# One sequence at a time in the compression stage of a hybrid decoder step, the first sequence's leading tokens asked for ahead of its others

## The chip, the core and the metric

The kernel runs on one core of one Trainium2 chip. The metric is the device time of one execution in microseconds (us): the kernel before takes 1231.15 us, the median of 3 runs (1231.12 to 1231.8). The core has four engines that compute, each with an instruction stream of its own: TensorE (PE in the profile; its weight loads are shown apart as PEld), VectorE (DVE), ScalarE (ACT) and GpSimd (POOL). SyncE (SP) only issues transfers here, and ACT and POOL can issue transfers too. The transfers of all three run on the same 16 DMA engines.

## The reference, cut to what matters

The whole program is one step of a decoder layer (two kinds of attention, gates, an MLP) for a prompt of 512 tokens and for 8 sample sequences, each with 2048 tokens in a paged cache of 16 pages of 128 tokens. The change touches the first stage alone, in which the cached raw keys and values of the 8 sequences are compressed:

```
def compress_blocks(x, pos, w1, w2):            # x: 8 x 2048 tokens x 2 groups x 64
    xc = x.reshape(b, n_chunk, 16, NSA_GROUPS, HEAD_DIM)          # chunks of 16 tokens
    w1 = w1.reshape(2, 16, HEAD_DIM, CMP_HIDDEN)                  # CMP_HIDDEN = 128
    lead  = einsum('bncgd,cdh->bngh', xc + pos[0], w1[0])
    trail = einsum('bncgd,cdh->bngh', xc + pos[1], w1[1])
    return einsum('bngh,hd->bngd', silu(lead[:, :-1] + trail[:, 1:]), w2)
```

It is done once for keys (`k`) and once for values (`v`), with a weight `w1` of 2048 x 128 each. The result is needed only in a later stage (the sample attention); what follows the first stage directly is the projection of the 576 new tokens by `w_in` (`z` in the profile).

## The kernel before, in words

**Data.** A sequence's pages are loaded into a tile `cpg` of 2 MB (16 loads of 128 KB, a page each; 4 such tiles, so that sequence b + 4 waits for the tile of sequence b). A page lies over 8 partition groups of 16 partitions, 8 tokens to a partition. The page's number in the cache is data: `by_page` (L157) first loads 8 page numbers into registers of the engine that issues (L162), then issues 8 loads (through `dma`, L151 to L155).

**Units.** The work is cut into units (L548) of one token place j (0 to 3; tokens 2j and 2j + 1 of each 8) and one of k or v. A unit of a sequence is made so:

- `cmp_order` (L447): DVE copies tokens 2j, 2j + 1 of a sequence into an order fit for transposing (`ro`; one copy serves k and v, so one for every two units).
- `rows_turn` (L456): four TensorE transposes (`ct`) into one PSUM bank, then twice ACT rounds half of it (`xh`) and DVE forms the remainder (`xl`), so that a product of full precision is had from three products of rounded numbers. Two `ring` buffers hold the results of two units.
- `cmp_hidden` (L473): 12 matmuls (`hid`) of the unit's `w1` parts with `xh` and `xl`, added up over all four j in PSUM.
- `cmp_taps` (L372), for the first eight units alone: ACT and DVE split the unit's part of `w1` in the same way (`w1hlk`, `w1hlv`, 128x512 each).

Before the change sequences 0 and 1 go through in units of one sequence (256 columns a matmul, units 0 to 15), and 2 to 7 in three pairs (512 columns, units 16 to 39; a pair's unit has two `ro` copies, eight transposes and four `xh` and `xl`).

**Order.** PE's order is the order of the program: every PE instruction is chained to the one before (`link`, L87). In the loop of `first_stage` (L623) it is: transposes of unit u + 1, matmuls of unit u, then whatever `todo[u]` holds: norms of the new tokens and their transposes (`norm`, `turned`; `nt` in the profile), the adaLN products (`ada_first`; `ada`, `adat`), the second weights of the compression (`cmp_act`, `cmp_out`, `cmp_keys`; `co`, `kct`), page loads of later sequences. On the other engines a planner orders what is not pinned; `behind()` (L535) pins an instruction behind the latest `xh` and `xl` of the program. The copy `ro` that opens a new sequence or pair is always so pinned, behind the `xh` and `xl` of the unit before it (L636 to L639). The other copies are pinned for units below 16 only.

**Transfers.** Each issuing engine's transfers go in the program's order (L153). At the start SP loads the page table, 8 pages of sequence 0, then sequences 1, 2 and 3; ACT loads `w1` of k (2 x 512 KB), the other 8 pages of sequence 0, then `w1` of v; POOL loads small constants.

**The seam.** At unit 38 of 40 `seam()` (L2095) opens the next stage: the first part of `w_in` (`winr`, two halves) is split into `winh`, `winl`, and the eight rows of the normed input into `h2_0` to `h2_7` (`split_pack`, one ACT and two DVE instructions each; `h` in the profile, L777). Rows 0 to 2 are pinned behind unit 38's `xl`, the others and both halves of `w_in` behind unit 39's. The first `z` tile needs all eight rows and both halves, in order.

Of the kernel before, what the change touches and what calls it, by code (L numbers as in the profile page):

```python
# [45 lines left out]
class Step:  # L46
# [465 lines left out]
    def first_stage(self, pl, pe, hf, seam):  # L512


        nc = self.nc
        self.chain = ""
        self.sideb = self.mmb
# [23 lines left out]
        def pinned(f):  # L541
            def g():
                with behind():
# [25 lines left out]
        ada, ends = [4, 0, 5, 1, 6, 2, 7, 3], {}  # L569
        todo = {u: [] for u in range(40)}  # L570
        todo[9] += [pinned(self.ada_silu)]
# [17 lines left out]

        todo[8] += [pages(4)]  # L590
        todo[9] += [asked(self.cmp_second)]
        todo[14] += [pages(5)]
        todo[15] += [asked(load_x)]
        todo[16] += [load_x, load_x]
        todo[17] += [asked(wada(0))]
        todo[19] += [load_x]
        todo[21] += [load_x]
        todo[23] += [asked(wada(1))]
        todo[24] += [self.late_loads]
        todo[20] += [pages(6)]  # L600
        todo[22] += [pages(7)]
        for k, u in enumerate((22, 25, 27, 29, 31, 32, 34, 35)):
            todo[u] += [lambda k=k: ends.update({k: self.ada_first(pe, ada[k])})]
            todo[u + 1] += [lambda k=k: ends[k]()]
            if k > 1:
                todo[(23, 26, 28, 30, 32, 33)[k - 2]] += [wada(k)]
            if k % 2:
                todo[max(u + 2, 28)] += [lambda k=k: self.modulate(0, hf, range(k - 1, k + 1))]
        self.lfg = {}
        for y, u in enumerate((25, 28)):  # L610
            todo[u] += [pinned(lambda y=y: self.stage_logf(pe, y))]
            todo[u + 2] += [lambda y=y: self.store_logf(y)]
        for i in range(3):
            for kv in range(2):
                todo[8 * i + 14 + kv] += [lambda i=i, kv=kv: self.cmp_act(pl, i, kv)]
        for i in range(3):
            for kv in range(2):
                todo[8 * i + 18 + kv] += [lambda i=i, kv=kv: self.cmp_out(pl, i, kv)]
            todo[8 * i + 21] += [lambda i=i: self.cmp_keys(i)]
        self.cmp_order(pl, 0)  # L620
        self.cmp_taps(0)
        self.rows_turn(0)
        for u in range(40):  # L623
            if u % 2 == 0 and u + 2 < 40 and (u + 2) % 8:
                with behind() if u + 2 < 16 else nullcontext():
                    self.cmp_order(pl, u + 2)
            if u + 1 < 8:
                with behind():
                    self.cmp_taps(u + 1)
            if u + 1 < 40:  # L630
# [5 lines left out]
            if (u + 2) % 8 == 0 and u + 2 < 40:  # L636

                with behind():
                    self.cmp_order(pl, u + 2)  # L639
# [1433 lines left out]
    def run(self):  # L2073
# [21 lines left out]
        def seam():  # L2095
# [158 lines left out]
```

## Time and profile before

| what | value |
|---|---|
| measured runs | 1231.12, 1231.15, 1231.8 us |
| the profiled execution | 1231.5 us |
| its span (first to last instruction) | 1229.7 us, 1.8 us less |
| granted TensorE clock, mean | 0.994 |
| first transposes of unit 0 | at 18.68 us |
| last `hid` matmul, begin of `z` | 170.66 and 170.88 us |
| moved to and from memory | 188.11 MB |

All times below are from the span's start. A row of a timeline has the start, the duration, engine, line, operation, what it writes <- what it reads, the number of instructions merged in the row and, in brackets, how long the engine had been idle and what released it. The chain of waits is followed back from the last instruction: each row is a start, a duration and what the end of the program was waiting for. A table by stretches has, for each stretch, the busy time of each engine with its number of instructions, the granted clock, the mean busy share of the DMA engines (shares over 1 come from overlapping packets) and GB/s. The duration of a matmul has its way through the array in it; what a stream of them costs is read from start to start.

### The profile page before, as it was taken

What the parts mean: (1) busy time and instruction counts of PE and PEld (TensorE: products, weight loads), DVE (VectorE), ACT (ScalarE), POOL (GpSimd) and SP (SyncE); (2) the same over time, 40 slices, a digit from 0 to 9 for tenths busy, and PEclk for the clock granted to TensorE, in tenths of its full rate; (3) what the DMA queues carried; (4) which work ended last, traced back from release to release, by engine and by line L of the source; (5) the groups of instructions that cost most, each with busy time, mean ns of one, the idle gap of its engine ahead of it and who ended that gap; (6) DMA issues with size and microseconds to landing.
All of it is one profiled execution on the core that took longest, in us unless ns stands there. A gap on an engine that the chain in (4) does not pass through costs nothing.

```text
span 1229.7 us, 24815 instructions
## 1 busy us (share of the span) xinstructions
PE 1186.9 (97%) x9475; PEld 1022.7 (83%) x9475; DVE 684.9 (56%) x1875; ACT 513.6 (42%) x1152; POOL 131.2 (11%) x144
## 2 busy tenths in 40 slices
PE   3899999999999989999999999999999999999998
PEld 3888789999666556666799999998989989899896
DVE  3688785676788845555543445654343433434546
ACT  2455453454777744454432333365423213232230
POOL 1012100001211120000200000001102011020110
PEclk9999999999999899999999999999999999999999
DMA  9589547794866449789763234115314223142202
GB/s 208 160 246 272 161 145 235 245 319 151 287 208 200 132 138 308 255 264 295 172 165 94 78 93 128 29 52 155 103 43 130 69 70 103 53 119 70 69 18 77
DMA packets 170201, 188.11 MB, mean 153 GB/s; under 512 B 16185, under 2 KB 149762, under 8 KB 167906
## 3 DMA queue, kind: packets, MB, share of 16 engines
q1 hardware_dynamic: 157890, 167.13, 44.6%
q0 software_dynamic: 6880, 16.25, 4.4%
q10 hardware_dynamic: 5312, 3.15, 1.2%
q8 instruction: 75, 1.23, 0.4%
q14 instruction: 44, 0.36, 0.1%
HBM read 176.48 MB, written 30.90 MB: 169 GB/s over the span
## 4 chain that ended last, share of the span: by engine, by line
PE 85%; DVE 5%; DMA 4%; SPq 3%; ACT 2%; issue 1%; DVEq 0%; ACTq 0%
PE up L77 17%; PE dn L77 17%; PE mg L77 8%; PE z L77 7%; PE hid L77 5%; PE wo L77 4%; PE br L77 4%; PE ss L77 4%; SPq L155 3%; PE k L83 2%; PE ct L83 2%; PE so L77 2%; DMA cpg<-in_cache_nsa_kv 2%; PE ada L77 1%; PE sp L83 1%
## 5 line engine op out<-in xcount | busy, mean ns | idle before, releaser
L77 PE MATMUL z<-winh,h 128*128 128x264 f32 (+1 forms) x576 | 111.0, 286 | 0.3
L2024 POOL TENSOR_TENSOR u<-u 128x576 f32<-128x576 f32 x32 | 53.4, 1669 | 409.3 <-ACT u L112 318.2
L77 PEld LDWEIGHTS z<-winh,h 128*128 128x128 f32 x576 | 91.7, 190 | 2.1 <-DVE h L777 0.9
L77 PE MATMUL z<-winl,h 128*128 128x264 f32 (+1 forms) x320 | 88.2, 284 | 0.2 <-DVE winl L131 0.2
L100 DVE TENSOR_TENSOR acc<-acc,dn 128x512 f32<-128x512 f32 x60 | 39.8, 685 | 73.0 <-PE dn L77 73.0
L77 PE MATMUL mg<-hH,wmh 128*128 128x288 f32 x256 | 75.9, 298 | 2.0 <-ACT wmh L112 2.0
L77 PE MATMUL mg<-hH,wml 128*128 128x288 f32 x256 | 75.9, 298 | 0.9 <-DVE wml L131 0.9
L112 ACT ACTIVATE xh<-ct 128x256 fp32r<-128x256 f32 x128 | 48.0, 385 | 59.2 <-PE ct L83 35.8
L77 PE MATMUL mg<-hL,wmh 128*128 128x288 f32 x256 | 72.6, 294 | 0.0
L131 DVE TENSOR_TENSOR xl<-ct,xh 128x256 fp32r<-128x256 f32 x128 | 51.6, 420 | 19.4 <-ACT xh L112 17.7
L777 DVE TENSOR_TENSOR u<-u,u 128x512 fp32r<-128x512 f32 x64 | 27.4, 469 | 60.7 <-ACT u L112 60.7
L77 PEld LDWEIGHTS z<-winl,h 128*128 128x128 f32 x320 | 60.6, 190 | 0.4 <-DVE winl L131 0.4
L83 PE MATMUL ct<-identF,ro 128*128 128x128 f32 x256 | 36.3, 281 | 22.7 <-DVE ro L115 22.1
L83 PEld LDWEIGHTS ct<-identF,ro 128*128 128x128 f32 x256 | 29.6, 146 | 26.6 <-DVE ro L115 18.7
L77 PEld LDWEIGHTS mg<-hH,wmh 128*128 128x128 f32 x256 | 48.6, 190 | 2.4 <-ACT wmh L112 2.2
L77 PEld LDWEIGHTS mg<-hH,wml 128*128 128x128 f32 x256 | 48.5, 189 | 1.1 <-DVE wml L131 1.1
L131 DVE TENSOR_TENSOR wml<-wmr,wmh 128x1024 fp32r<-128x1024 f32 x14 | 17.1, 1224 | 56.0 <-ACT wmh L112 55.9
L112 ACT ACTIVATE u<-up 128x256 f32<-128x256 f32 (+1 forms) x96 | 27.8, 325 | 48.7 <-PE up L77 48.7
L77 PEld LDWEIGHTS mg<-hL,wmh 128*128 128x128 f32 x256 | 47.2, 188 | 0.1
L77 PE MATMUL hid<-xh,w1hlk 128*128 128x512 f32 (+1 forms) x160 | 45.0, 369 | 0.1
L77 PE MATMUL hid<-xh,w1hlv 128*128 128x512 f32 (+1 forms) x160 | 43.9, 360 | 0.5 <-ACT xh L112 0.5
L1700 DVE CUSTOM_DVE_ANT_0 sS<-ss,scr 128x512 f32<-128x512 f32 x32 | 22.1, 691 | 30.2 <-PE ss L77 30.2
(951 smaller groups left out, 3584.1 us busy)
## 6 DMA issues: line engine op xcount, KB each, us to landing
adw<-in_w_ada SPq DMA_DIRECT2D x16, 1024.0 KB
foxD<-in_cache_fox_kv SPq DMA_DIRECT2D x128, 128.0 KB
wur<-in_w_up SPq DMA_DIRECT2D x32, 512.0 KB
wdr<-in_w_down SPq DMA_DIRECT2D x32, 512.0 KB
cpg<-in_cache_nsa_kv SPq DMA_DIRECT2D x120, 128.0 KB
fr<-foxD SPq DMA_DIRECT2D x28, 512.0 KB
sr<-in_cache_nsa_kv SPq DMA_DIRECT2D x112, 128.0 KB
wada<-in_w_ada POOLq DMA_DIRECT2D x8, 1024.0 KB, 6.3
```

The costliest lines, as they stand in the source:

```text
L77: ins = self.nc.tensor.matmul(out, a, b, start=start, stop=stop, skip_group_check=True)
L83: ins = self.nc.tensor.transpose(out, in_, self.identF[:n, :n])
L100: self.nc.vector.tensor_tensor(out, a, b, op=op)
L112: return self.nc.scalar.activation(out, in_, f, **kw)
L131: self.splits.append((eng or self.nc.vector).tensor_tensor(l, x, h.bitcast(F32), op=OP.subtract).ins)
L155: self.issued[eng] = getattr(self.nc, eng).dma_start(out, in_).ins
L777: self.packed = (eng or self.nc.vector).tensor_tensor(h2[:, o:o + n], x[:, i:i + n], h2[:, i:i + n].bitcast(F32), op=OP.subtract).ins
L1700: self.nc.vector.tensor_tensor_reduce(self.S[u], pb, self.ramp[:, 512 * i:512 * i + 512], 1.0, LOW, OP.add, OP.max, self.stat[b][0][:, i / ...
L2024: nc.gpsimd.tensor_tensor(u[j], u[j], u[j], op=OP.mult)
```

## The change

All 8 sequences become units of one sequence: 64 units of 256 columns instead of 16 of 256 and 24 of 512. `w1` is loaded by token place (8 loads of 256 KB instead of 4 of 512 KB): places 0 and 1 by ACT, 2 and 3 by POOL. Of sequence 0 the first two tokens of each page's 8 are asked for first (SP and ACT, 8 pages each, 32 KB a load), the other six after (SP and POOL, 96 KB a load). The copies `ro` are all pinned behind the latest `xl`. The entries of `todo` are moved to the new numbering. At the seam, now at unit 62 of 64, row 0 is pinned behind unit 61's `xl`, row 1 behind unit 62's, the others behind unit 63's.

```diff
@@ by_page
-                    engines=[{"sync": mybir.EngineType.SP, "scalar": mybir.EngineType.Activation}[eng]],
+                    engines=[{"sync": mybir.EngineType.SP, "scalar": mybir.EngineType.Activation,
+                              "gpsimd": mybir.EngineType.Pool}[eng]],
@@ cmp_raw
-        n = "kv"[kv]
-        raw = pe.tile([P, 16, P], F32, tag="big", bufs=2, name=f"w1raw{n}")
-        for j in (0, 8):
-            self.dma("scalar", raw[:, j:j + 8], self.I[f"cmp_w1_{n}"][0, P * j:P * j + D].rearrange("(j p) h -> p j h", p=P))
-        self.w1raw.append(raw)
+        self.w1raw.append(pe.tile([P, 16, P], F32, tag="big", bufs=2, name=f"w1raw{kv}"))
+
+    def cmp_raw_taps(self, kv, js, eng="scalar"):
+        v = self.I[f"cmp_w1_{'kv'[kv]}"][0].rearrange("(a j p) h -> j p a h", a=4, p=P)
+        for j in js:
+            self.dma(eng, self.w1raw[kv].rearrange("p (a j) h -> p a j h", a=4)[:, :, j], v[j])
@@ first_stage
-        self.units = [(b // 2, bs, j, kv) for b, bs in ((0, (0,)), (1, (1,)), (2, (2, 3)), (4, (4, 5)), (6, (6, 7)))
-                      for j in range(4) for kv in range(2)]
+        self.units = [(b // 2, (b,), j, kv) for b in range(NB) for j in range(4) for kv in range(2)]
+        N = len(self.units)
...
-        self.cmp_raw(pe, 0)
+        for kv in range(2):
+            self.cmp_raw(pe, kv)
+            self.cmp_raw_taps(kv, (0,))
...
-        self.cmp_pages("sync", 0, slice(0, 8))
-        self.cmp_pages("scalar", 0, slice(8, 16))
-        self.cmp_raw(pe, 1)
+        self.cmp_pages("sync", 0, slice(0, 8), slice(0, 2))
+        self.cmp_pages("scalar", 0, slice(8, 16), slice(0, 2))
+        self.cmp_pages("gpsimd", 0, slice(8, 16), slice(2, 8))
+        self.cmp_pages("sync", 0, slice(0, 8), slice(2, 8))
+        for j in range(1, 4):
+            for kv in range(2):
+                self.cmp_raw_taps(kv, (j,), "scalar" if j == 1 else "gpsimd")
...
-        for k, u in enumerate((19, 21, 23, 25, 27)):
-            todo[u - 2] += [lambda k=k: norm(k)]
+        for k, u in enumerate((22, 26, 30, 34, 38)):
+            todo[u - 3] += [lambda k=k: norm(k)]
             todo[u] += [lambda k=k: turned(k)]
...
-        for k, u in enumerate((22, 25, 27, 29, 31, 32, 34, 35)):
+        for k, u in enumerate((29, 34, 39, 43, 47, 50, 53, 56)):
             todo[u] += [lambda k=k: ends.update({k: self.ada_first(pe, ada[k])})]
             todo[u + 1] += [lambda k=k: ends[k]()]
...
-                todo[8 * i + 14 + kv] += [lambda i=i, kv=kv: self.cmp_act(pl, i, kv)]
+                todo[16 * i + 14 + kv] += [lambda i=i, kv=kv: self.cmp_act(pl, i, kv)]
...
-        for u in range(40):
-            if u % 2 == 0 and u + 2 < 40 and (u + 2) % 8:
-                with behind() if u + 2 < 16 else nullcontext():
+        for u in range(N):
+            if u % 2 == 0 and u + 2 < N and (u + 2) % 8:
+                with behind():
                     self.cmp_order(pl, u + 2)
...
-            if u == 37:
-                self.behind38 = self.splits[-1], self.last_high
-            if u == 38:
+            if N - 4 <= u < N - 2:
+                self.ahead.append((self.splits[-1], self.last_high))
+            if u == N - 2:
                 seam()
@@ run, in seam
-            rows(self.behind38, range(3))
+            rows(self.ahead[0], (0,))
+            rows(self.ahead[1], (1,))
             for i in range(2):
                 self.win_split(self.pw, 0, i, last)
-                rows(last, ((3, 4), (5, 6, 7))[i])
+                rows(last, ((2, 3, 4), (5, 6, 7))[i])
```

The cut lines move the other loads of `todo` (pages of sequences 4 to 7 at units 8, 14, 22, 30 instead of 8, 14, 20, 22; the input rows, the adaLN weights, the forget values) in the same way.

More of the change, by code (lines that the diff above doesn't have):

```diff
@@ L515, in first_stage @@
         nc = self.nc
-        self.chain = ""
+        self.chain, self.ahead = "", []
         self.sideb = self.mmb
@@ L569, in first_stage @@
         ada, ends = [4, 0, 5, 1, 6, 2, 7, 3], {}
-        todo = {u: [] for u in range(40)}
+        todo = {u: [] for u in range(N)}
         todo[9] += [pinned(self.ada_silu)]
@@ L588, in asked @@
             return g
-        todo[8] += [pages(4)]
+        for b in range(4, NB):
+            todo[8 * (b - 4) + (8 if b == 4 else 6)] += [pages(b)]
         todo[9] += [asked(self.cmp_second)]
-        todo[14] += [pages(5)]
         todo[15] += [asked(load_x)]
[L594 to L601, printed above, removed]
-        for k, u in enumerate((22, 25, 27, 29, 31, 32, 34, 35)):
+        todo[16] += [load_x]
+        todo[18] += [load_x]
+        todo[20] += [asked(wada(0))]
+        todo[23] += [load_x]
+        todo[25] += [asked(wada(1))]
+        todo[27] += [load_x]
+        todo[28] += [self.late_loads]
+        for k, u in enumerate((29, 34, 39, 43, 47, 50, 53, 56)):
             todo[u] += [lambda k=k: ends.update({k: self.ada_first(pe, ada[k])})]
             todo[u + 1] += [lambda k=k: ends[k]()]
-            if k > 1:
-                todo[(23, 26, 28, 30, 32, 33)[k - 2]] += [wada(k)]
+            if k < 6:
+                todo[u + 1] += [wada(k + 2)]
             if k % 2:
-                todo[max(u + 2, 28)] += [lambda k=k: self.modulate(0, hf, range(k - 1, k + 1))]
+                todo[max(u + 2, 40)] += [lambda k=k: self.modulate(0, hf, range(k - 1, k + 1))]
         self.lfg = {}
-        for y, u in enumerate((25, 28)):
+        for y, u in enumerate((36, 41)):
             todo[u] += [pinned(lambda y=y: self.stage_logf(pe, y))]
-            todo[u + 2] += [lambda y=y: self.store_logf(y)]
+            todo[u + 4] += [lambda y=y: self.store_logf(y)]
         for i in range(3):
             for kv in range(2):
-                todo[8 * i + 14 + kv] += [lambda i=i, kv=kv: self.cmp_act(pl, i, kv)]
+                todo[16 * i + 14 + kv] += [lambda i=i, kv=kv: self.cmp_act(pl, i, kv)]
         for i in range(3):
             for kv in range(2):
-                todo[8 * i + 18 + kv] += [lambda i=i, kv=kv: self.cmp_out(pl, i, kv)]
-            todo[8 * i + 21] += [lambda i=i: self.cmp_keys(i)]
+                todo[16 * i + 18 + kv] += [lambda i=i, kv=kv: self.cmp_out(pl, i, kv)]
+            todo[16 * i + 21] += [lambda i=i: self.cmp_keys(i)]
         self.cmp_order(pl, 0)
@@ L629, in first_stage @@
                     self.cmp_taps(u + 1)
-            if u + 1 < 40:
+            if u + 1 < N:
                 self.rows_turn(u + 1)
-            if u == 37:
-                self.behind38 = self.splits[-1], self.last_high
-            if u == 38:
+            if N - 4 <= u < N - 2:
+                self.ahead.append((self.splits[-1], self.last_high))
+            if u == N - 2:
                 seam()
-            if (u + 2) % 8 == 0 and u + 2 < 40:
+            if (u + 2) % 8 == 0 and u + 2 < N:
                 with behind():
```

## The prediction

> **What bounds the kernel now.** I read the shares of the chain of waits first, then the stage's stretches, then the chain through them.
>
> ```profile
> PE 85%; DVE 5%; DMA 4%; SPq 3%; ACT 2%; issue 1%; DVEq 0%; ACTq 0%
> ```
> ```profile
> 4.00:26.00 22.00, 7.18 (x36) 6.65 (x37) 5.31 (x11) 4.20 (x10) 2.92 (x6) 1.00 1.15 235
> 26.00:58.00 32.00, 28.92 (x289) 27.63 (x288) 20.00 (x47) 14.43 (x35) 1.30 (x3) 1.00 0.54 158
> 61.64:171.06 109.42, 109.11 (x712) 87.96 (x713) 87.62 (x304) 56.66 (x135) 15.43 (x21) 1.00 0.71 201
> ```
> ```profile
> 2.95 0.72 SPq L155
> 3.86 6.62 DMA cpg<-in_cache_nsa_kv
> ...
> 28.21 0.58 SPq L155
> ...
> 53.90 0.54 SPq L155
> 54.62 0.54 SPq L155
> 55.35 2.65 DMA cpg<-in_cache_nsa_kv
> 58.39 0.52 DVE ro L115
> ...
> 61.64 1.06 PE ct L83 x8
> ...
> 77.79 0.87 PE nt L83 x8
> ...
> 83.19 0.87 PE ct L83 x8
> 84.06 2.79 PE hid L77 x12
> ...
> 96.43 0.45 PE nt L83 x4
> ```
>
> PE is the bound, but not at first. Until 26 us the DMA engines are full (share 1.15). Until 55 us SP asks for one page each 0.72 us, and the first pair waits for sequence 3's last page. From 61.64 to 171.06 PE is busy for 109.11 of 109.42 us: there only more work or a new gap on PE can change the end. A pair's unit costs 0.87 + 2.79 = 3.66 us.
>
> **The change part by part.** First the units of one sequence and the starts of sequences, on PE (first two fences, the first from the opening stretch, the second later) and on DVE:
>
> ```profile
> 18.68 1.97 PE L83 MATMUL ct<-identF,ro 128*128 128x128 f32 x8 [18.68 <-DVE ro L115]
> ...
> 23.57 0.85 PE L83 MATMUL ct<-identF,ro 128*128 128x128 f32 x4
> ...
> 26.01 0.60 PE L83 MATMUL ct<-identF,ro 128*128 128x128 f32 x4
> ```
> ```profile
> 34.53 0.60 PE L83 MATMUL ct<-identF,ro 128*128 128x128 f32 x4
> ...
> 38.06 0.63 PE L83 MATMUL ct<-identF,ro 128*128 128x128 f32 x4 [1.48 <-DVE ro L115]
> 39.94 0.60 PE L83 MATMUL ct<-identF,ro 128*128 128x128 f32 x4
> ...
> 43.71 0.60 PE L83 MATMUL ct<-identF,ro 128*128 128x128 f32 x4
> ```
> ```profile
> 54.61 0.60 PE L83 MATMUL ct<-identF,ro 128*128 128x128 f32 x4
> ...
> 57.80 0.63 PE L83 MATMUL ct<-identF,ro 128*128 128x128 f32 x4 [1.14 <-DVE ro L115]
> 59.23 0.63 PE L83 MATMUL ct<-identF,ro 128*128 128x128 f32 x4 [0.79 <-DVE ro L115]
> ```
> ```profile
> 56.60 0.42 DVE L131 TENSOR_TENSOR xl<-ct,xh 128x256 fp32r<-128x256 f32 x1 [0.45 <-ACT xh L112]
> 56.97 0.69 DVE L115 COPY ro<-cpg 128x1024 f32<-128x1024 f32 x1
> ```
>
> *Width.* From 39.94 to 43.71 two single units take 3.77 us against 3.66 for a pair's: 24 x 0.11 = 2.6 us more, and one set of four transposes (0.44, half of 0.87) is still to come at the point from which I count (unit 17's transposes, begun at 61.64 before): **+3.1**. ACT and DVE instructions stay the same in number.
>
> *Front.* Before, unit 0 starts at 18.68, when all of sequence 0 and k's `w1` have landed, some 3.1 MB. Units 2 to 7 need these same bytes still (sequence 0, and places 0 and 1 of `w1`), at the same full DMA engines; SP's 16 shorter loads take it to 2.95 + 16 x 0.72 + 0.7 for page numbers = 15.2 us, and a landing behind that (2.65 at 55.35, 6.62 at 3.86), 17.9 to 21.8. Unit 0 and perhaps 1 go ahead of it: 2.95 + 8 x 0.72 + 2.65 + 0.7 for `ro` is 12 us at the earliest. So unit 2's transposes start at 18.7 to 22.5 instead of 23.57 (in the first rows above; unit 3 followed at 26.01, a pitch and a wait for v's `w1` later): I take 20.4, a gain of 3.2, and 0.4 for that wait: **-3.6**, bounds -1.5 and -5.5. SP's eight more loads cost nothing while it waits for full DMA engines anyway (24 loads until 28.21 are 1.05 us each); with that cover gone they would cost 8 x 0.72 = 5.8 us, sequence 1 would land at 28.8 + 2.65 + 5.8 = 37 instead of 31, and unit 8, due at 34.4, would take back all of the gain. POOL's eight page loads and four of `w1` go ahead of its constants, each at 0.5 to 0.9 us by these rows, so some 11 us and one wait; the constants are needed at 45. A page load by POOL with a register the trace doesn't show: 0.5 to 2 us each, and 0.5, the nearest row, is taken; at 2 the tokens of pages 8 to 15 come at 21, which is the range's end above.
>
> ```profile
> 8.29 0.52 POOL L155 DMA_DIRECT2D gains<-in_nsa_qn_g  x1 [2.40 <-DMA adw<-in_c_prompt]
> ...
> 67.84 0.92 POOL L155 DMA_DIRECT2D wada<-in_w_ada  x1 [0.45 <-ACT xh L112]
> ```
>
> The Trainium skill ("DMA: Bandwidth & Descriptors", "Issuing engines are not separate DMA queues") says that transfers started from several engines share the same 16 and that this saves only the time of asking. The share of 1.15 until 26 us agrees. By that rule alone the front would give nothing, and the sum below would be 3.6 us higher; it is a rival below.
>
> *The wait for sequence 3.* Unit 16 needs sequence 2 alone. Before, unit 16 starts at 57.80 and unit 17 at 61.64; now 1.88 later: 3.84 - 1.88 = **-2.0**. Sequences 3 to 7 then have 13 us each of asking for 17 of PE, so SP isn't late again.
>
> *The gap at each new sequence.* The copy that opens a sequence stands behind the last `xl`: 54.61 transposes, 56.60 `xl`, 56.97 `ro`, 57.80 next transposes. That is 3.19 us where the steady pitch is 1.88, a gap of 1.3 on PE; from 34.53 to 38.06 it is even 3.53. A pair hid it behind 2.79 us of matmuls; now there are only 1.44 (1.88 - 0.44). Five more such starts follow (units 22, 30, 38, 46, 54). What `todo` holds there fills part: 0.87 at 22, 0.87 and 0.22 at 30, 0.45 at 38, 0.22 at 54, nothing at 46 (the 0.22 is half of the 0.45 row, two transposes for four). What is left: 0.43 + 0.21 + 0.85 + 1.3 + 1.08 = 3.9; before lost some 0.6 at pairs: **+3.3**, bounds 0 and 6.
>
> *Chain within a unit.* Transposes, `xh`, `xl`, `xh`, `xl` last from 54.61 to 57.0, 2.4 us. They must end before the next unit's sixth matmul, 1.88 + 0.36 + 0.6 = 2.84 later, so a DVE or ACT instruction over some 0.4 us between them reaches PE; a pair had over 1 us. What comes between:
>
> ```profile
> L131 DVE TENSOR_TENSOR xl<-ct,xh 128x256 fp32r<-128x256 f32 x93 | 37.2, 419 | 5.5 <-ACT xh L112 4.0
> L115 DVE COPY ro<-cpg 128x1024 f32<-128x1024 f32 x21 | 14.6, 712 | 1.0 <-PE ct L83 0.9
> ```
>
> DVE's 87.6 us less 96 x 0.42 and 24 x 0.70 are 30 us of other work over 48 units, 0.64 us each. Bounds: with 0.69 us of DVE and 0.62 of ACT more per unit (the `w1` splits), 26.01 to 34.53 took 8.52 for four units instead of 7.54, 0.25 a unit: 48 x 0.25 = 12. From 38.06 to 54.61, seven units with 3.2 us of other PE work, it cost 0.1 in all: 0. PE's other work, 109.4 - 87 = 22 us, gives the chain time in many units, but not where norms, `cmp_act` and the modulation of rows fall. I take 30% of the upper end: **+3.5**.
>
> *Seam.* DVE's rows around it, then PE's:
>
> ```profile
> 168.57 1.26 DVE L131 TENSOR_TENSOR winl<-winr,winh 128x1056 fp32r<-128x1056 f32 x1 [0.55 <-ACT winh L112]
> 169.75 1.56 DVE L777 TENSOR_TENSOR h<-adw,h 128x512 fp32r<-128x512 f32 x4
> 171.23 1.25 DVE L131 TENSOR_TENSOR winl<-winr,winh 128x1056 fp32r<-128x1056 f32 x1
> 172.40 2.29 DVE L777 TENSOR_TENSOR h<-adw,h 128x512 fp32r<-128x512 f32 x6
> ```
> ```profile
> 164.43 1.03 PE L83 MATMUL ct<-identF,ro 128*128 128x128 f32 x8
> ...
> 170.88 0.40 PE L77 MATMUL z<-winh,h 128*128 128x264 f32 x2
> ...
> 174.95 0.41 PE L77 MATMUL z<-winh,h 128*128 128x264 f32 x2
> ```
>
> ```profile
> 178.87 2.96 PE z L77 x24
> ```
>
> The first `z` tile lasts from 170.88 to 174.95, 4.07 us; its 24 matmuls need 2.96, as the chain's row of a later tile shows: 1.1 lost to `h`. Behind the last `xl` DVE now has both `winl` and six rows: 2.41 + 0.55 + 1.26 + 2.3 + 1.25 + 2.3 = 10.1 us after the last transposes, about as before. But PE has only hid 62 and 63 left, and is done 3.3 us after them, not 6.45. The tile ends at 10.3, so 4.05 are lost, **+3.0**, bounds 0 and 4.
>
> *Sum:* -3.6 - 2.0 + 3.1 + 3.3 + 3.5 + 3.0 = +7.3. The profiled execution took 1231.5 (span 1229.7, 1.8 around it) and becomes 1238.8; it stood 0.35 above the median, so **1238.5 us**.
>
> **Rivals.**
>
> 1. *Three engines bring nothing at the front.* The bytes of unit 2 come no earlier. For: the full DMA engines. Against: unit 0's own start-up, 18.68 to 23.57, moves ahead in any case. The front is 0: 1242.1.
> 2. *DVE becomes the bound.* It is busy for 80% from 61.64 on, and gaps cost the upper 12 us: 1247. Against: `todo` is spread thinner, over 64 units.
> 3. *PE doesn't starve between the first unit and the third sequence* (faster). The place is 18.68 to 61.64: 43 us for 16 units (30.1), 3.2 of constants and 0.9 of a pair's transposes leave 8.8 lost; with units 0 and 1 ahead, 3.8 more: 12.6 gained, not 5.6. It decides if the first unit of sequence 1 starts before about 30 us (34.4 in my forecast). With the chain within a unit at 0 as well, -12.6 + 3.1 + 3.3 + 3.0 = -3.2: 1228. Against: the gaps at 38.06 and 57.80 are pins in the code, not transfers.
> 4. *The new gaps are covered, the front is as forecast:* at the starts and within units 0, the sum is +0.5: 1231.7.
>
> **How the numbers follow.** Forecast 0.40 (1235 to 1241), rival 1 0.18, rival 2 0.12, rival 3 0.18, rival 4 0.12. A measurement of this kernel tells about 0.2%, 2.5 us, from no change. Slower by more is 0.40 + 0.18 + 0.12 = 0.70, within it rival 4, 0.12, faster rival 3, 0.18. The range 1228 to 1246 leaves out most of what is faster still and half of rival 2.
>
> **What would show it.** Unit 0 at 12 to 13 us and unit 2 at about 20.4: the front. Transposes at the start of sequences 3, 5, 6 and 7 held up by `ro` for about a microsecond: the gap. PE idle before `hid` and `xl` as releaser in units 16 to 63: the chain. A first `z` tile of 7 us instead of 4.07: the seam. The last `hid` at about 175 us, and 1.88 us from unit to unit. I am wrong if PE stays without gaps from unit 16 on, or if sequence 1 starts well before 34 us.

## The result and the profile after

The kernel after takes **1246.18 us**, the median of 4 runs (1244.04 to 1246.8), against 1231.13 (1228.1 to 1231.8) for the kernel before: the ratio is **1.0124, with a 95% interval of 1.0103 to 1.0145**. The forecast was 1238.5 with a range of 1228 to 1246: slower, as forecast, but by twice as much, and just outside the range. The profiled execution took 1246.07 us, with a span of 1244.4, which is 14.7 us more than the span before.

First the shares of the chain of waits after (asking by SP has 5% of it instead of 3), then the table by stretches, then the first transposes of units 0, 2, 3, 8, 16 and 17 and of unit 48 (sequence 6's first) in the timeline of TensorE (PE).

```profile
PE 82%; SPq 5%; DVE 5%; DMA 4%; ACT 2%; issue 2%; DVEq 0%; ACTq 0%
```
```profile
4.00:26.00 22.00, 6.70 (x31) 6.20 (x32) 5.22 (x10) 3.63 (x9) 12.87 (x22) 0.88 0.80 208
26.00:58.00 32.00, 30.01 (x292) 28.70 (x290) 19.72 (x47) 14.05 (x35) 1.33 (x3) 0.98 0.56 160
60.66:181.44 120.78, 114.00 (x1005) 105.30 (x1004) 88.69 (x303) 55.92 (x134) 16.17 (x22) 1.00 0.67 187
```
```profile
13.60 1.97 PE L83 MATMUL ct<-identF,ro 128*128 128x128 f32 x8 [13.60 <-DVE ro L115]
23.68 1.08 PE L83 MATMUL ct<-identF,ro 128*128 128x128 f32 x4 [5.61 <-DVE ro L115]
27.12 0.73 PE L83 MATMUL ct<-identF,ro 128*128 128x128 f32 x4
...
38.97 0.63 PE L83 MATMUL ct<-identF,ro 128*128 128x128 f32 x4 [1.13 <-DVE ro L115]
...
58.76 0.63 PE L83 MATMUL ct<-identF,ro 128*128 128x128 f32 x4 [1.15 <-DVE ro L115]
60.66 0.60 PE L83 MATMUL ct<-identF,ro 128*128 128x128 f32 x4
...
140.07 0.63 PE L83 MATMUL ct<-identF,ro 128*128 128x128 f32 x4 [1.15 <-DVE ro L115]
```

Unit 0 starts five microseconds earlier than before, at 13.60, and nothing comes of it: PE then waits 5.61 us, unit 2 starts at 23.68 (23.57 before) and unit 16 at 58.76 (57.80 before). Until 26 us the DMA engines are less busy than before (0.80 against 1.15), so the front isn't held by full DMA engines throughout. From unit 17 to `z` the kernel needs 120.78 us where it needed 109.24, and PE is idle for 6.8 us of it, where it had been idle for 0.3.

The seam, in the rows of PE (idle time in brackets) and the stretches behind it:

```profile
181.44 0.41 PE L77 MATMUL z<-winh,h 128*128 128x264 f32 x2
182.49 0.39 PE L77 MATMUL z<-winl,h 128*128 128x264 f32 x1 [0.65 <-DVE winl L131]
...
185.87 0.39 PE L77 MATMUL z<-winl,h 128*128 128x264 f32 x1 [0.91 <-DVE winl L131]
...
188.55 0.65 PE L77 MATMUL z<-winh,h 128*128 128x264 f32 x2
```
```profile
186.00:188.00 2.00, 1.70 (x9) 1.07 (x9) 2.00 (x7) 1.83 (x4) 0.00 (x0) 0.95 0.88 234
188.00:190.00 2.00, 2.00 (x9) 2.00 (x10) 2.00 (x3) 1.45 (x3) 0.00 (x0) 0.50 1.10 385
190.00:192.00 2.00, 2.00 (x14) 2.00 (x13) 0.96 (x2) 0.97 (x2) 0.00 (x0) 0.69 0.88 312
192.00:194.00 2.00, 2.00 (x19) 2.00 (x19) 1.06 (x3) 0.64 (x2) 0.00 (x0) 1.00 0.66 192
```

The first `z` tile lasts 7 us, as forecast. What follows wasn't forecast: the granted clock falls to 0.50, and a stretch of 2 us holds 9 matmuls instead of 18 or 19.

Where the 14.7 us are, each step from the start of a row before to the same row after:

| step | forecast | measured |
|---|---|---|
| front (start of unit 16, 57.80 to 58.76) | -3.6 | **+0.96** |
| wait for sequence 3 (unit 16 to 17, 3.84 to 1.90) | -2.0 | -1.94 |
| unit 17 to the first `z` (109.24 to 120.78): width, starts, chain | +9.9 | **+11.54** |
| first `z` tile, 24 matmuls (4.07 to 7.11) | +3.0 | +3.04 |
| the 96 `z` matmuls behind it (14.56 to 15.77) | 0 | +1.21 |
| from there to the end | 0 | -0.16 |

Two of these had to be explained: the front, 4.6 us off, and the middle.

### The profile page after: what moved, and what is told of

The parts are those of the page before. It is cut to its first block, busy times and chain, and to the rows that moved or that the text cites. A ratio compares the mean times of both kernels' runs of the same rounds, so it can differ in the third digit from the quotient of the medians.

```text
span 1244.4 us, 25438 instructions
## 1 busy us (share of the span) xinstructions
PE 1194.6 (96%) x9763; PEld 1042.2 (84%) x9763; DVE 687.5 (55%) x1875; ACT 515.1 (41%) x1152; POOL 139.0 (11%) x156
## 4 chain that ended last, share of the span: by engine, by line
PE 82%; SPq 5%; DVE 5%; DMA 4%; ACT 2%; issue 2%; DVEq 0%; ACTq 0%
PE up L77 16%; PE dn L77 16%; PE z L77 9%; PE mg L77 8%; SPq L155 4%; PE wo L77 4%; PE br L77 4%; PE ss L77 3%; DMA cpg<-in_cache_nsa_kv 3%; PE hid L77 2%; PE k L83 2%; PE so L77 2%; PE ada L77 2%; PE sp L83 1%; PE ct L83 1%
## 5 line engine op out<-in xcount | busy, mean ns | idle before, releaser
L83 PE MATMUL ct<-identF,ro 128*128 128x128 f32 x256 | 40.4, 283 | 24.8 <-DVE ro L115 23.8
L77 PE MATMUL hid<-xh,w1hlv 128*128 128x256 f32 x256 | 51.4, 297 | 0.5 <-ACT xh L112 0.5
L77 PE MATMUL hid<-xh,w1hlk 128*128 128x256 f32 x256 | 51.3, 298 | 0.1
L77 PEld LDWEIGHTS hid<-xh,w1hlv 128*128 128x128 f32 x256 | 40.2, 194 | 0.9 <-ACT xh L112 0.9
```

The source lines that it names most:

```text
L77: ins = self.nc.tensor.matmul(out, a, b, start=start, stop=stop, skip_group_check=True)
L83: ins = self.nc.tensor.transpose(out, in_, self.identF[:n, :n])
```

## The experiments

All ratios are against runs of the kernel before on the same chip. Behind the 120th `z` matmul the code is the same in all these kernels, yet the profiles take from 1035.5 to 1041.9 us there. So steps are read from the rows of the first stage, and a difference of a few microseconds between the times of two kernels shows little by itself.

### The front

My theory after the result: the 1 MB of `w1`'s places 2 and 3, which GpSimd (POOL) asks for in these rows, go ahead of the rest of sequence 0. The rival: the order of asking makes no difference, as rival 1 of the prediction had it.

```profile
8.46 0.79 POOL L155 DMA_DIRECT2D w1raw<-in_cmp_w_k  x1
...
10.71 0.75 POOL L155 DMA_DIRECT2D w1raw<-in_cmp_w_v  x1
```

**SP asks for that part of `w1` instead, behind sequence 0.**

```diff
-                self.cmp_raw_taps(kv, (j,), "scalar" if j == 1 else "gpsimd")
+                self.cmp_raw_taps(kv, (j,), "scalar" if j == 1 else "sync")
```


> The changed kernel with w1's places 2 and 3 asked for by SP behind all of sequence 0's pages, instead of by POOL beside them. Theory A (the 1 MB of w1 takes the DMA engines while SP's last pages of sequence 0 wait): unit 2's transposes start at about 20.4 us instead of 23.68, the TensorE clock stays at 1.00 between 20 and 28 us, the time falls by 4 to 5 us to about 1241.5. Rival (SP's doubled number of loads, of which only some may be under way, makes the last pages late): unit 2 stays at 23 to 24 us, the time at 1246 or, with sequence 1 asked for 2.9 us later, up to 1249.

1243.92 us, ratio 1.0109 (1.0091 to 1.0127). The first transposes of units 2, 8 and 9:

```profile
19.31 0.63 PE L83 MATMUL ct<-identF,ro 128*128 128x128 f32 x4 [1.31 <-DVE ro L115]
...
35.78 1.09 PE L83 MATMUL ct<-identF,ro 128*128 128x128 f32 x4 [3.70 <-DVE ro L115]
39.22 1.05 PE L83 MATMUL ct<-identF,ro 128*128 128x128 f32 x4
```

Unit 2 comes 4.4 us earlier, as the theory says. But SP, which now has four more loads ahead of sequence 1, brings that one late: unit 8 waits 3.70 us, unit 9 follows at half rate, and unit 16 starts at 58.00.

**The new order with the loads of before**, and **the kernel before with the new loads alone** (the same edit the other way round).

```diff
-            self.cmp_raw_taps(kv, (0,))
+        self.cmp_raw_half(0)
...
-        self.cmp_pages("sync", 0, slice(0, 8), slice(0, 2))
...
+        self.cmp_pages("sync", 0, slice(0, 8))
+        self.cmp_pages("scalar", 0, slice(8, 16))
+        self.cmp_raw_half(1)
```

> The changed kernel with the loads of before at the start (w1 in halves by ACT, 8 whole pages by SP and 8 by ACT); units of one sequence and the seam stay changed. Theory: the new front is worth -1 us at best, since unit 2 starts at 23.6 in both and the changed kernel pays a halved clock behind its gap: unit 16 starts at about 57.8 instead of 58.76, the time is 1245, the rest of the 15 us being made behind unit 16. Rival (the front gains what was forecast, and the loss lies elsewhere): 1249 to 1250.

> The kernel before with the changed loads at the start alone; units and pairs as before. Theory: the halved clock from 21 to 27 us appears here too, unit 2 starts at 23.7 and unit 16 at 58.8; the first pair waits for sequence 3's last page, which is asked for 3 us later (58.5 instead of 55.35), so 1233 to 1235. Rival (the early first units do gain): 1229 or less.

The first: 1242.4 us, 1.0099 (1.0082 to 1.0115), less than either expectation, with unit 16 at 58.04, 0.7 earlier than with the new loads. That is no clear difference: two kernels below with the same front as the kernel after, those with more time for the small chains and with a pair at the end, have unit 16 at 57.88 and 59.18. And `z` begins only 0.67 earlier; of the 4.7 us between the two profiles 2.6 are from behind the 120th `z` matmul. The second: 1235.53 us, 1.0042 (1.0027 to 1.0058), unit 16 at 58.22. There the cost comes behind it, as expected: the pair waits for sequence 3's page, and `z` begins at 175.89 instead of 170.88.

```profile
62.54 1.09 PE L83 MATMUL ct<-identF,ro 128*128 128x128 f32 x4 [3.69 <-DVE ro L115]
```

So the new loads as they are gain nothing in the new order of units, and cost in the old one.

**GpSimd asks for half of sequence 1** (on top of the first experiment).

```diff
-        self.cmp_pages("sync", 1)
+        self.cmp_pages("gpsimd", 1, slice(8, 16))
+        self.cmp_pages("sync", 1, slice(0, 8))
```


> The kernel after with w1's places 2 and 3 asked for by SP behind sequence 0's pages, and eight of sequence 1's sixteen pages asked for by GpSimd instead of SP. Theory (SP's asking, one load after another, is what made unit 8 wait 3.7 us for sequence 1 once unit 2 came early): unit 8 at about 33 us, unit 16 at about 54 instead of 58.0, 1239 to 1241 us. Rival (the bytes bound it, whoever asks): unit 8 at 35 us or later, unit 16 at 57 or later, 1243 to 1244 us.

1246.37 us, 1.0127 (1.0099 to 1.0156): unit 2 is back at 24.02 and unit 8 at 39.95. Against my expectation, and instructive: these pages are 1 MB as well, and POOL again asked for them at once.

**GpSimd asks for `w1`'s places 2 and 3 only once unit 1's `xl` is there.**

```diff
+        def late_taps():
+            c = nc.gpsimd.tensor_copy(warm, self.ring[1][1][:, 0, 0:1].bitcast(F32))
+            with self.tc.issue_after(c.ins):
+                for j in (2, 3):
+                    for kv in range(2):
+                        self.cmp_raw_taps(kv, (j,), "gpsimd")
+        todo[0] += [late_taps]
```


> The kernel after, but GpSimd asks for w1's places 2 and 3 (1 MB) only once unit 1's xl is there, at about 16.5 us instead of 8.5. Theory (the order of the bytes decides): unit 2 at 19 to 20.5 us instead of 23.68 and, as SP has nothing else to ask for, sequence 1 in time: unit 8 at 34 to 36 us instead of 38.97, unit 16 at 54 to 55.5 instead of 58.76, 1241 to 1242.5 us. Rival (the bytes in all, or the limit of loads under way on SP, decide): unit 8 still at 38 us or later, unit 16 at 57.5 or later, 1244 us or more.

1239.61 us, 1.0075 (1.0051 to 1.0098), 6.6 us below the kernel after. The transposes of units 0, 2, 3, 8, 9 and 16, and POOL's first load of `w1`:

```profile
13.31 1.97 PE L83 MATMUL ct<-identF,ro 128*128 128x128 f32 x8 [13.31 <-DVE ro L115]
19.45 0.63 PE L83 MATMUL ct<-identF,ro 128*128 128x128 f32 x4 [1.77 <-DVE ro L115]
21.35 0.60 PE L83 MATMUL ct<-identF,ro 128*128 128x128 f32 x4
...
33.70 0.63 PE L83 MATMUL ct<-identF,ro 128*128 128x128 f32 x4 [1.50 <-DVE ro L115]
35.59 0.60 PE L83 MATMUL ct<-identF,ro 128*128 128x128 f32 x4
...
53.45 0.63 PE L83 MATMUL ct<-identF,ro 128*128 128x128 f32 x4 [1.14 <-DVE ro L115]
```
```profile
16.45 0.83 POOL L155 DMA_DIRECT2D w1raw<-in_cmp_w_k  x1
```

Unit 16 starts 5.3 us earlier than after and 4.35 earlier than before; the front then gives what was forecast, and more. The table of the DMA queues from 8 to 16 us shows why (q0 is POOL's queue, q1 SP's, q10 ACT's; packets, MB, share of the 16 engines' time), first of the kernel after, then of this one:

```profile
q0 software_dynamic: 461, 1.30, 57.5%
q10 hardware_dynamic: 1147, 0.61, 28.9%
q1 hardware_dynamic: 291, 0.22, 13.1%
```
```profile
q1 hardware_dynamic: 840, 0.70, 36.8%
q10 hardware_dynamic: 1251, 0.66, 30.8%
q0 software_dynamic: 499, 0.43, 20.4%
```

The DMA engines are nearly full in both (99.5% and 88.0%). After, SP's queue moves 0.22 MB in these 8 us, and with POOL's loads of `w1` out of the way 0.70. The Trainium skill ("DMA: Bandwidth & Descriptors", "Queues, rings and completion order") says that each DMA engine takes turns between the queues that have work for it, packet by packet; the rows agree that an early request of another engine isn't put behind SP's but shares with it.

### The middle

The theory was the forecast's: gaps at new sequences, and the chain from transposes to the last `xl` within a unit. The rival: VectorE (DVE) is the bound.

**The opening copies of a sequence placed like all others**, two units ahead (in the kernel after, then in the kernel before for units 8 and 16).

```diff
-            if u % 2 == 0 and u + 2 < N and (u + 2) % 8:
+            if u % 2 == 0 and u + 2 < N:
...
-            if (u + 2) % 8 == 0 and u + 2 < N:
-                with behind():
-                    self.cmp_order(pl, u + 2)
```


> The changed kernel with the copy that opens a sequence placed like all the others, ahead of the next unit's xl instead of behind them. Theory (the gap at each new sequence is that pin): PE's waits for ro at units 8, 16, 24, 40, 48 and 56 vanish, 5 to 6.5 us less, 1240 to 1241. Rival (the copy then stands in the chain of the unit before and PE waits there instead): under 2 us less, 1244 to 1246.

> The kernel before with the copies that open sequence 1 and the first pair (units 8 and 16) placed like all others, nothing else changed. Theory: unit 8 starts 1.3 us sooner (36.8), unit 16 about 2.5 sooner, but the pair waits for sequence 3's last page at 58.4 as before, so unit 17 stays at 61 to 61.6: 1230 to 1231. Rival (SP isn't the bound there): -2.5, 1228.5.

After: 1241.05 us, 1.009 (1.0076 to 1.0104). Units 8 and 16 come 1.6 and 2.2 us earlier (0.6 of it at unit 2 already, which the edit doesn't touch), but from unit 17 to `z` only 1.4 are won, although the pitches (from one unit's transposes to the next's) at the starts of sequences 3 to 7 shrink by 3.6 in sum: 2.2 us come back as longer pitches at other places. In the kernel before: 1232.38 us, 1.0016 (1.0003 to 1.0029); unit 16 is ready at 55.26, and PE then waits 4.50 us, since DVE's copy for the other half of the pair waits for sequence 3's page until 58.30. There the pin costs nothing, since the page is later still.

**Three ring buffers, transposes two units ahead**, with the copies early; then the same with the loads of before.

```diff
-        for i in range(2):
+        for i in range(3):
...
-        xh, xl = self.ring[u % 2]
+        xh, xl = self.ring[u % 3]
...
-            if u + 1 < N:
-                self.rows_turn(u + 1)
+            if u + 2 < N:
+                self.rows_turn(u + 2)
```


> The kernel after with three ring buffers instead of two, transposes issued two units ahead of their matmuls, and the copy that opens a sequence placed a unit earlier. Theory (the middle is lost in the chain of transposes, xh and xl within a unit, which the ring of two leaves too little time): from unit 17 to the first z tile 112 to 114 us instead of 120.8, pitches of about 1.88 between units with nothing else in them, no gaps put down to ro or xl, the first z tile 5.5 to 6.9 us, 1236 to 1238 us. Rival (VectorE's whole load bounds the stretch, so a deeper ring only moves the wait): from unit 17 to z 118 to 120 us, 1239 to 1241 us, no better than with the early copy alone (1241.05).

> The same deeper ring with the loads of the kernel before at the start (w1 in halves of 512 KB by ScalarE, sequence 0 whole, nothing by GpSimd). If the new front costs about 1.5 us, as the run with the old loads alone said: unit 17 and all behind it 1 to 2 us earlier than in the deeper ring with the new front, 1234 to 1236 us. Rival (with transposes two units ahead the new loads do bring unit 2 forward): this one is 1 to 3 us slower than the deeper ring with the new front.

1240.58 us, 1.0086 (1.0056 to 1.0116), and 1239.12 us, 1.0068 (1.0046 to 1.0089). From unit 16's first `hid` matmul to `z` (the ruler for all that follows) the kernel after takes 120.43 us (five others with the same middle 120.1 to 120.6), the early copies 119.04, the deeper ring 116.20: less than the theory's gain. With the loads of before unit 16's `hid` comes a microsecond earlier (59.97 for 60.96), as two units ahead unit 2's transposes stand before `hid` of unit 0 too, and nothing is left of the early start. What PE waits for there (in total, times, longest), in the kernel after and with the deeper ring:

```profile
PE ct L83 <- DVE ro L115: 2.3, 3, 1.1
PE nt L83 <- DVE x L104: 1.4, 2, 0.8
PE kct L83 <- DVE ntt L100: 1.0, 1, 1.0
PE ct L83 <- DVE adas L309: 0.9, 1, 0.9
PE co L77 <- DVE w2rawk L104: 0.5, 1, 0.5
PE kct L83 <- DVE knn L100: 0.4, 1, 0.4
...
```
```profile
PE nt L83 <- DVE x L104: 2.0, 2, 1.6
PE kct L83 <- DVE nrs L109: 0.9, 1, 0.9
PE ct L83 <- DVE ntt L100: 0.8, 2, 0.7
...
```

The waits for `ro` are gone; those for the small chains of `todo` (norms `x`, `ntt`, `nrs`; the second weights; the adaLN sums `adas`) stay. These chains have fixed places in PE's order.

**More units of time for these chains**: first in the kernel after, then with the deeper ring and the early copies.

```diff
-            todo[u - 3] += [lambda k=k: norm(k)]
+            todo[u - 5] += [lambda k=k: norm(k)]
...
-        todo[18] += [pinned(self.cmp_second_half)]
+        todo[15] += [pinned(self.cmp_second_half)]
...
-            todo[u + 1] += [lambda k=k: ends[k]()]
+            todo[u + 2] += [lambda k=k: ends[k]()]
...
-            todo[16 * i + 21] += [lambda i=i: self.cmp_keys(i)]
+            todo[16 * i + 25] += [lambda i=i: self.cmp_keys(i)]
```


> The kernel after with more units of time for the small chains on which TensorE waits: norms five units ahead of their transposes instead of three, the second weights halved three units earlier, the adaLN ends one unit and cmp_keys four units later; the work is the same. Theory (4.2 us of the middle are these waits, since fixed places in the order of 1.88 us units leave less time than places in 3.66 us units): waits for x, ntt, knn, w2rawk and adas under 1 us in all, from unit 17 to z 117 to 118 us instead of 120.8, 1242.5 to 1244 us. Rival (VectorE is behind there in any case, and the wait moves to xl or ro): from unit 17 to z 120 us or more, 1245 to 1247 us.

> The kernel after with the ring of three and transposes two units ahead, the opening copies early, and in addition the small chains given more units of time as in the run with slack alone. Theory (TensorE waits for these chains because of their places in its order, and depth is needed so that the wait doesn't move to xl): from unit 16's first matmul to z 112 to 114 us instead of 116.2, visible idle time of TensorE there under 2.5 us instead of 4.6, 1237 to 1238.5 us. Rival (VectorE's load and the planner's order on it decide, not the places): 115.5 to 117.5 us again, 1239 to 1241 us.

| kernel | unit 16's `hid` to `z` | PE idle in it | time, ratio |
|---|---|---|---|
| after | 120.43 | 6.78 | 1246.18, 1.0124 (1.0103 to 1.0145) |
| more time alone | 121.42 | 5.17 | 1243.99, 1.0111 (1.0091 to 1.013) |
| early copies | 119.04 | 5.23 | 1241.05, 1.009 (1.0076 to 1.0104) |
| early copies, ring of three | 116.20 | 4.58 | 1240.58, 1.0086 (1.0056 to 1.0116) |
| all three | **111.34** | **0.62** | 1232.67, 1.0008 (0.9994 to 1.0022) |

The rows of the last two kernels of the table by stretches, the ring of three first:

```profile
60.96:177.16 116.20, 111.62 (x998) 104.04 (x996) 86.89 (x301) 54.67 (x132) 13.46 (x19) 1.00 0.70 192
```
```profile
60.11:171.45 111.34, 110.72 (x997) 104.01 (x996) 85.73 (x301) 53.99 (x132) 13.92 (x19) 1.00 0.72 197
```

More time alone gives nothing: PE's waits for these chains vanish, and 3.8 us of waits for `ro` and 0.9 for `xh` take their place. Together with depth it gives 4.9 us, more than I expected. DVE does much the same work in the quickest kernel (85.73 us of 111.34) as in the slower ones (86.89 of 116.20), so its load isn't the bound; the rival falls.

### The seam and the clock

**Sequences 6 and 7 as a pair**, with rows 0 to 2 pinned as before the change (lines not shown move three adaLN entries of `todo` forward and leave the pair's other copies unpinned).

```diff
-        self.units = [(b // 2, (b,), j, kv) for b in range(NB) for j in range(4) for kv in range(2)]
+        self.units = [(bs[0] // 2, bs, j, kv) for bs in [(b,) for b in range(6)] + [(6, 7)] for j in range(4) for kv in range(2)]
...
-            rows(self.ahead[0], (0,))
-            rows(self.ahead[1], (1,))
+            rows(self.ahead[0], range(3))
```


> The changed kernel with sequences 6 and 7 as a pair again (units 48 to 55), and the seam pinned as before; the front as changed. Theory: the first z tile takes 4 us instead of 7 (-3), PE isn't idle there long enough to lose its clock (-1.2), one gap at a new sequence is gone (-1.1) and width gives -0.9: z starts at 179 instead of 181.4, the time is 1240 to 1241. Rival (the seam was not short of matmuls to cover it, DVE is simply late): 1244 to 1245.

1238.04 us, 1.0053 (1.0031 to 1.0075). The first `z` tile takes 4.10 us again: the seam's 3.0 us are due to the single unit that covers it, as forecast.

**46 transposes of the identity into an unused tile**, in PE's gap ahead of unit 2 (work is added, none left out).

```diff
+        fill = self.mmb("fill")
+        todo[0] += [lambda: [self.tr(fill[:, 0:P], self.identF) for _ in range(46)]]
```


> The changed kernel with 46 transposes of the identity added behind unit 0's matmuls, into a PSUM bank that nothing reads: they fill PE's empty 5.6 us before unit 2 and delay nothing that is ready. Theory (the empty stretch halves the TensorE clock, and unit 2 pays for it): the clock stays 1.00 from 20 to 28 us, unit 3 starts 2.4 us after unit 2 instead of 3.44, the time falls by 1.0 to 1.4 to 1245. Rival (the clock drops for another reason, or unit 2 is slow because w1 is late): unit 3 still 3.4 us behind unit 2, 1246.

Stretches of the kernel after, then of this one (the clock is the third number from the end):

```profile
22.00:24.00 2.00, 0.32 (x2) 0.35 (x3) 0.69 (x1) 0.00 (x0) 0.00 (x0) 0.50 0.57 155
24.00:26.00 2.00, 2.00 (x11) 2.00 (x10) 0.42 (x1) 0.65 (x2) 0.00 (x0) 0.50 0.58 186
```
```profile
24.00:26.00 2.00, 2.00 (x20) 2.00 (x18) 0.42 (x1) 0.64 (x2) 0.00 (x0) 1.00 0.62 180
```

With the gap filled PE does 20 matmuls in 2 us instead of 11, and unit 3 follows unit 2 in 1.87 us instead of 3.44. So the half rate behind the gap comes from the gap. It is worth little here: unit 2 itself starts 0.5 later, right behind the last added transpose, unit 17 0.9 earlier, and the time is 1246.55 us, 1.0131 (1.0111 to 1.0151), no less than after.

### A version under both kernels?

Sequences 0 to 3 one by one and 4 to 7 as two pairs, opening copies early, loads of before unless said. The edits, against the kernel before, in the order of the table (not shown: the entries of `todo` under their new numbers and the copies that open a sequence); the fourth is that of the late `w1` above, the fifth is its `cmp_pages("gpsimd", 1, slice(8, 16))` behind these loads:

```diff
-        ... (2, (2, 3)), (4, (4, 5)), (6, (6, 7)))
+        ... (2, (2,)), (3, (3,)), (4, (4, 5)), (6, (6, 7)))
...
+    def slot(self, u):
+        if u < 32:
+            return *self.ring[u % 4 // 2], 258 * (u % 2)
+        return *self.ring[u % 2], 0
...
+            if u <= 9 or 32 <= u + 1 < 48:
+                self.rows_turn(u + 1)
+            if 9 <= u < 30:
+                self.rows_turn(u + 2)
```

| kernel | unit 16's `hid` | `z` begins | time, ratio |
|---|---|---|---|
| mixed | 56.99 | 172.87 | 1234.24, 1.0028 (1.0015 to 1.0041) |
| and four half buffers, two units ahead | 58.22 | 169.20 | 1231.93, 1.0015 (0.9998 to 1.0031) |
| two ahead only from unit 9 | 57.72 | 169.17 | 1230.94, 1.0006 (0.9995 to 1.0017) |
| and the new loads with late `w1` | 57.16 | 169.44 | 1232.11, 1.001 (0.9999 to 1.0021) |
| and POOL asks for half of sequence 1 | 58.40 | 174.96 | 1233.44, 1.0016 (1.0003 to 1.0029) |

> The kernel before, its front kept, with sequences 0 to 3 in units of one and 4 to 7 in two pairs, and the copies that open sequences 1, 2 and 3 placed like all others: what of the change can gain without what costs. Theory: unit 16 at 55.3, unit 17 at 57.2 without a wait for sequence 3; eight pairs' units as sixteen single ones cost 1.3 and their tighter chain 1 to 2; z starts at 168 to 169.5 instead of 170.9, the time is 1229 to 1230. Rival (single units cost more in their chain than the wait that they save): 1232 or more.

> Loads of the kernel before, sequences 0 to 3 one by one and 4 to 7 as two pairs, the opening copies early (the mixed kernel of 1234.24 us), and in addition four half buffers with the transposes of single units two units ahead. Theory (single units lose to the chain within a unit): z starts at 168 to 170 us instead of 172.87, 1229 to 1231 us, level with the kernel before or a little faster. Rival (the loss is VectorE's load or other work): z at 172 to 173 us, 1233 to 1235 us.

> The same mixed kernel with the start of the kernel before. Theory (the first units lost 1.3 us when transposes stood two units ahead from the beginning, the rest is as in the mixed deeper kernel): unit 16 at 54.8 us, z at 167.5 to 168.5 us instead of 169.2, 1229 to 1230.5 us. Rival (the time from unit 16 on depends on how the buffers stand then): z at 169 to 171 us, 1231 to 1233 us.

> The mixed kernel (sequences 0 to 3 one by one, 4 to 7 as two pairs, four half buffers, opening copies early), with transposes two units ahead only from unit 9 on, and with the start of the kernel after, GpSimd's w1 places 2 and 3 asked for after unit 1. If the order of the bytes decides the front and depth the middle: unit 8 at 34 to 36 us, unit 16 at 52 to 54, z at 164 to 167 us, 1225 to 1228 us, faster than before. Rival (the front gives nothing here): unit 16 at 55 or later, z at 168 or later, 1229 to 1231 us.

> The mixed kernel with the new start and GpSimd's late w1, in which GpSimd also asks for eight of sequence 1's sixteen pages behind these. Theory (SP's asking keeps unit 8, which waits until 34.07 there and is followed by 2.4 us at half rate): unit 8 at 31.5 to 32.5 us, no half rate behind it, z at 165.5 to 167 us, 1227.5 to 1229.5 us, under the kernel before. Rival (the bytes of w1 and sequence 1 keep it): unit 8 at 33.5 us or later, z at 169 to 170 us, 1231 to 1233 us.

The second is the only theory here that held, by the begin of `z` (the time is 0.9 us above its range): depth brings `z` 3.7 us forward. The other four missed, and no version is faster than before. With the late `w1` unit 2 starts at 19.53, but sequence 1 is then what is late. Units 7, 8 and 9 of that kernel:

```profile
30.17 0.60 PE L83 MATMUL ct<-identF,ro 128*128 128x128 f32 x4
34.07 0.67 PE L83 MATMUL ct<-identF,ro 128*128 128x128 f32 x4 [1.85 <-DVE ro L115]
37.45 0.84 PE L83 MATMUL ct<-identF,ro 128*128 128x128 f32 x4
```

Unit 9 follows in 3.38 us where it took 1.89 in the late-`w1` kernel above (33.70 to 35.59): the half rate takes the gain back. With POOL's pages unit 8 comes at 35.67, so SP's asking isn't what is short. That kernel then takes 116.56 us to `z` where the one without takes 112.28, and the loss is in one place: units 34 and 35 take 5.9 us more. DVE waits there for a small load of the page table (`ptT`), which POOL asked for at 96.79 and 95.85 (first the kernel with POOL's pages, then the one without):

```profile
108.70 0.15 DVE L106 TENSOR_SCALAR lfrow<-ptT 128x1 int32<-128x1 int32 x1 [5.75 <-DMA ptT<-in_page_table]
```
```profile
104.20 0.15 DVE L106 TENSOR_SCALAR lfrow<-ptT 128x1 int32<-128x1 int32 x1 [1.32 <-DMA ptT<-in_page_table]
```

With POOL's pages PE then waits 1.95 us for DVE's copy `adap` of an adaLN product and 0.91 for `nrs` of a norm, and runs at half rate behind them. Why the load takes longer there stays open; in the kernel before, DVE waits 1.25 us for it too.

All three repairs of the middle together with the late `w1` weren't tried in one kernel.

## Why the prediction was wrong in size

**The front is the step that failed.** It said that units 2 to 7 "need these same bytes still (sequence 0, and places 0 and 1 of `w1`)", and that POOL's loads cost nothing but POOL's own time: they "go ahead of its constants". I counted POOL's loads as instructions (its page loads took 0.59 us each, 8 in 4.70, near the 0.5 that I took) and left out the bytes of `w1`. Places 2 and 3 aren't needed before unit 4, but they were asked for at 8.46 us and took turns with SP's pages. Putting off only that moved unit 16 from 58.76 to 53.45, which puts the term at -4.35 instead of +0.96 (forecast -3.6, bounds -1.5 and -5.5). The prediction's own remark that transfers of several engines share the same 16 pointed there: read as "the front would give nothing", it became rival 1; its use was to ask whose bytes go first. Rival 1's time was nearer, but its reason, full DMA engines, was half the matter: from 8 to 16 us they were full, but in good part with bytes that weren't due, and with the order put right the front gains.

**The wait for sequence 3** (-1.94 for -2.0) and **the seam** (+3.04 for +3.0) were right, the seam also in its mechanism, by the pair at the end. But what a gap of PE at the seam does to the rate behind it was not in the sum: +1.21.

**The middle** was +11.54 for +9.9. *Width:* with all three repairs 111.34 us are left on the ruler. To compare with before, 0.36 for the one unit's transposes that stand ahead of it there, and 0.35 between the two rulers (120.78 and 120.43), have to be added: 112.05, that is 2.8 over before, for 3.1 forecast. The rest, 8.7, was forecast as 3.3 + 3.5. *Gaps at new sequences* were there as described (1.15 us at 140.07), but taking the pins away gave 1.4. *Chain within a unit:* the ring's depth gave 2.5 (2.84, less the 0.36). What I had not named are the waits for the small chains of `todo`, 4.9 together with the ring. I had taken PE's other work as something that "gives the chain time"; it also stands in PE's order and waits for DVE itself. So it is in part luck that 3.3 + 3.5 came near 8.7: the two named terms are worth 3.9. Places given in units were moved to new numbers, and a unit shrank from 3.66 to 1.88 us. Shown is that depth alone gives 2.8 us, more time alone nothing (tried without the early copies), and both together 7.7 (119.04 to 111.34); which of the moved chains counts most was not separated.

**Rival 2** (1247) came close to the time for the wrong reason, as DVE's load isn't the bound. **Rival 3's** condition, sequence 1 before 30 us, wasn't met even with the late `w1` (33.70). **Rival 4's** covered gaps exist only with the deeper ring and more time for the small chains, which the change doesn't have.

## What to carry to other kernels

When loads are moved to another engine's queue, count their bytes against those that are due first, not only the instructions that ask: an early request of one engine slows the urgent ones of another, and a tiny operation that only waits can put it in its place. When units of work get shorter, everything that was placed by counting units loses time with them: put the distances back in microseconds and give the ring another buffer, both at once, since either alone gave little here. And a stall on PE has to be priced with the half rate that can follow it.

## What the hardware did that I hadn't expected

Behind a gap PE can run at half rate, for about 3.4 us or twice that. In the mixed kernel in which POOL asks for half of sequence 1, matmuls start every 0.21 us instead of every 0.12 from 36.37 to 39.77, behind a wait of 2.47 us, and half rate lasts from 111.5 to 118.3, behind one of 1.95. The size of the longest gap alone doesn't decide it: with 1.77 us ahead of unit 2 the next unit followed in 1.90 us (late `w1`), and at the seam, where no wait is longer than 0.91 us but PE is idle for 2 of 7 us, half rate follows.

PE also begins the stage at half rate, and when that ends differs from kernel to kernel. With the late `w1` matmuls start every 0.21 us from unit 0 on and every 0.12 from 16.8. In the mixed kernel with POOL's pages they start every 0.21 us until 22.67, so that unit 2 takes 3.44 us though the wait ahead of it is short:

```profile
19.23 1.08 PE L83 MATMUL ct<-identF,ro 128*128 128x128 f32 x4 [1.04 <-DVE ro L115]
22.67 0.63 PE L83 MATMUL ct<-identF,ro 128*128 128x128 f32 x4
```

The granted clock doesn't always show it: it is 1.00 there from 20 to 22 us, with 11 matmuls in these 2 us.

The Trainium skill ("TensorE: Matmul & The Clock Gate", "Part 1: The HAM clock gate") has windows of 3.4 us that run on their own, half rate after an idle one and full after a busy one. The length agrees, and so does it that gaps of much the same size may or may not count (1.77 and 1.95 us). That a window has to be idle throughout doesn't agree: at the seam none was. In the kernel with the filled gap full rate sets in at 19.85 us, among the 46 transposes, and holds through 4.2 us of transposes alone.
